# Delta-rule diagonal blocks inverted by columns on VectorE, with block doubling from 16

## The chip, the cores and the metric

The kernel runs on one core of a Trainium2 chip. The metric is the device time of one execution in microseconds (us), as the median of several runs. The profile that is read below comes from one further execution of the same program.

## What is computed

The reference is one mixer layer over 2048 tokens of width 1024. A normalised input goes through one projection. Half of its columns feed a gated delta rule (4 heads of 128), the other half feed differential softmax attention (4 heads). Both outputs are gated, concatenated and projected back to the residual stream. The change touches only the delta rule's triangular solve:

```
m    = where(strict, einsum('bhncd,bhnsd->bhncs', k_beta, kc) * decay, 0)
lmat = m + eye(CHUNK)
sol  = triangular_solve(lmat, rhs, left_side=True, lower=True, unit_diagonal=True)
u, w = sol[..., :dv], sol[..., dv:]
```

The kernel works with chunks of 128 tokens. It forms the inverse of the unit-triangular matrix explicitly and multiplies by it.

## The kernel before

The program has two stages. In the first, TensorE projects the input (the products named `pct` and `pnat`, each of them split into high and low parts, so three products for one), and beside this the delta rule runs. In the second, attention runs beside the output projection (`outp`).

The delta rule is cut into 16 units: 4 heads h by 4 token groups g of 512 tokens, each with 4 chunks (`NCH`). Two chains of units run abreast, one for even and one for odd groups, so that the two units of one head and one half of the tokens go through together; here they are called a pair, and there are 8 pairs. A third chain, the scans, carries the state from chunk to chunk.

`gdn_unit` builds the strictly upper triangle `U` of a unit, transposes it on TensorE (`lp`) into `L`, and then inverts. It starts with the inverse `N` of the 2x2 diagonal blocks, which needs only a mask, and doubles the block size at each level: a product with `Lr` (`xp`), masked by VectorE into `X`, a product with `TT` (`np`), which VectorE subtracts from `N`, and a transposition of `N` on TensorE (`tp`), which ScalarE copies into `TT`. With `LEVELS = [1, 2, 4, 8, 16, 32, 64]` there are six such rounds, for 2 to 64. One residual step (`rp`, `R`, `cp`, `NF`) follows, and then the products with keys and values (`wp`, `ubp`).

The order on TensorE is made by `mingle`, which takes one step of the delta rule at a time and puts steps of the projections behind it, on average `RATE` of them for each step, so that TensorE has work while the delta rule waits for the other engines. A projection step may be moved forward past at most `SLACK` = 4 delta-rule steps; within that freedom the framework's scheduler fixes the order of each engine's queue when the program is built. Each engine then works through its queue in order.

SyncE issues nearly all transfers, in one queue and in order. GpSimd (POOL) does the subtractions that make the low parts of the weights (`wl_...`), some elementwise work, and a few transfers at the start.

Of the kernel before, what the change touches and what calls it, by code (L numbers as in the profile page):

```python
# [10 lines left out]
F32 = mybir.dt.float32  # L11
F32R = mybir.dt.float32r
AF = mybir.ActivationFunctionType
ALU = mybir.AluOpType
AX = mybir.AxisListType

P = 128
# [6 lines left out]
NCH = 4  # L24
# [9 lines left out]
LD = 3  # L34
WB = 4
ORDER = ((0, 0, 1, 1), (0, 0, 1, 1))
RATE = 5.25
RATE_T = 5.25
RATE_D = 5.25
SLACK = 4  # L40
LOWER = [(h, g) for h in (0, 1, 2, 3) for g in (0, 1, 2, 3)]
LASTG = (4, 5, 6, 7)
# [22 lines left out]
EXB = 14  # L65
WTB = 4

LEVELS = [1, 2, 4, 8, 16, 32, 64]


def level_masks():
    s = np.arange(P)[:, None]
    c = np.arange(P)[None, :]
    m = [((s // (2 * b) == c // (2 * b)) & (s // b % 2 == 0) & (c // b % 2 == 1)) for b in LEVELS]
    return np.ascontiguousarray(np.stack(m, 1).astype(np.float32))


def f(ap):
    return ap.bitcast(F32)
# [3 lines left out]
def hybrid_kernel(  # L83
# [20 lines left out]
    nc = tc.nc  # L104
    V, A, PL, SY = nc.vector, nc.scalar, nc.gpsimd, nc.sync
# [41 lines left out]
    const = ctx.enter_context(tc.tile_pool(name="const", bufs=1))  # L147
    dram = ctx.enter_context(tc.tile_pool(name="dram", bufs=1, space=bass.MemoryType.DRAM))
# [6 lines left out]
    def qt_(name):  # L155
        return psf.tile([P, NCH, P], F32, tag="qt", name=name, bufs=1)
# [12 lines left out]
    mx_d = [[dram.tile([2, 8, P, G], F32, name=f"mx_d{g}")] for g in range(T // G)]  # L169
    zdn_d = [dram.tile([P, T], F32, name=f"zdn_d{h}") for h in range(H)]  # L170
    part_d = [dram.tile([P, D], F32, name=f"part_d{i}") for i in range(T // P)]
    gc_d = [dram.tile([H, 8, P], F32, name=f"gc_d{i}") for i in range(2)]

    xp = p1.enter_context(tc.tile_pool(name="xp", bufs=1))
# [2 lines left out]
    gp = pg.enter_context(tc.tile_pool(name="gp", bufs=1, side="right"))  # L177
# [51 lines left out]
    ident = const.tile([P, P], F32, name="ident")  # L229
# [4 lines left out]
    V.memset(ones, 1.0)  # L234
    utri = const.tile([P, P], F32, name="utri")
    PL.affine_select(utri, ones, pattern=[[1, P]], compare_op=ALU.is_ge, fill=0.0, base=0, channel_multiplier=-1)
    lmask = const.tile([P, 7, P], F32, name="lmask")
    ab = const.tile([P, 2, H], F32, name="ab")
    nea = const.tile([P, H], F32, name="nea")
    dtb = ab[:, 1, :]  # L240
    lv = const.tile([P, 1], F32, name="lv")

    ngp = qt_("ngp")
    PE.transpose(ngp[:, 0, 0:8], ngt, ident[0:8, 0:8])
    ngain = const.tile([P, 8], F32, name="ngain")
# [46 lines left out]
    def ua(gg, name, dt=F32):  # L292
        return psg.tile([P, NCH, P], dt, tag=f"ua{gg}", name=name, bufs=1)
# [263 lines left out]
    solved = [0]  # L557
    scanned = [0]

    def gdn_unit(h, g):  # L560
        u = units.pop((h, g))
        hf, gg = g // 2, g % 2
        kq, vT = u["kq"], u["vT"]
        s = {k: a[:, h, 4 * gg : 4 * gg + 4] for k, a in sc[hf].items()}

        def t(tag, name, dt=F32, shape=S4):
            return gp.tile(shape, dt, tag=f"u{gg}_{tag}", name=f"u{gg}_{name}")

        def live(name):
# [5 lines left out]
            out=gcr.rearrange("p a b -> p (a b)"),  # L575
            in_=gc_d[hf][h, 4 * gg : 4 * gg + 4, :].rearrange("a b -> (a b)").partition_broadcast(P),
# [46 lines left out]
        U = t("d", "U")  # L623
# [13 lines left out]
        passed[0] += 1  # L637


        lp = ua(gg, "lp")  # L640
        for j in range(NCH):
            PE.transpose(lp[:, j, :], U[:, j, :], ident)
        idb = bc(ident.unsqueeze(1), S4)
        L = t("a", "L")
        V.tensor_tensor(L, lp, idb, op=ALU.add)
        Lr = t("b", "Lr", F32R)
        A.copy(Lr, L)

        def lm(i):
            return bc(lmask[:, i, :].unsqueeze(1), S4)  # L650

        n0 = t("e", "n0")
        PL.tensor_tensor(n0, U, lm(0), op=ALU.mult)
        N = t("c", "N", F32R)
        PL.tensor_tensor(N, idb, n0, op=ALU.subtract)

        def transposed(N):
            tp = ua(gg, "tp", F32R)
# [5 lines left out]

        TT = transposed(N)
        yield
        for i in range(1, 7):

            def odd(a):
                return a.rearrange("p j (m two b) -> p j m two b", two=2, b=LEVELS[i])[:, :, :, 1, :]  # L670

            def blocks(a):
                return a.rearrange("p j (m b) -> p j m b", b=LEVELS[i])

            No = odd(N)
            HC = P // 2
            xp_ = ua(gg, "xp")[:, :, :HC]
            for j in range(NCH):
                PE.matmul(xp_[:, j, :], lhsT=Lr[:, j, :], rhs=No[:, j], start=True, stop=True)
            X = t("e", "X", F32R)[:, :, :HC]  # L680
            V.tensor_tensor(blocks(X), blocks(xp_), odd(lm(i)), op=ALU.mult)
            yield
            np_ = ua(gg, "np")[:, :, :HC]
            for j in range(NCH):
                PE.matmul(np_[:, j, :], lhsT=TT[:, j, :], rhs=X[:, j, :], start=True, stop=True)
            V.tensor_tensor(No, f(No), blocks(np_), op=ALU.subtract)
            yield
            TT = transposed(N)
            yield
# [101 lines left out]

    pace = [RATE]

    def feed():

        for hf in range(2):
# [23 lines left out]
            if hf:  # L820
                pace[0] = RATE_T
            for r in rest:
# [439 lines left out]
def build(arrays):  # L1262
    import concourse.bacc as _bacc

    nc = _bacc.Bacc("TRN2", target_bir_lowering=False, num_devices=1)
    args = []
    for name, a in arrays.items():
        args.append(nc.dram_tensor(name, a.shape, mybir.dt.from_np(a.dtype), kind="ExternalInput").ap())
    args.append(nc.dram_tensor("out_0_dram", (1, T, D), F32, kind="ExternalOutput").ap())
    with tile.TileContext(nc, schedule_with_timeline_sim=True) as tc:  # L1270
        hybrid_kernel(tc, *args)
    return nc
# [10 lines left out]
```

## Time and profile before

| what | value |
|---|---|
| median of 3 runs | 1722.77 us (1721.42 to 1725.84) |
| the profiled execution | 1718.26 us |
| its span, first to last instruction | 1716.1 us |
| mean granted TensorE clock, share of full speed | 0.984 |
| busy, share of the span: TensorE products | 95% |
| VectorE, ScalarE, POOL | 62%, 44%, 40% |

The profiled execution took 2.2 us more than its span, and 4.5 us less than the median of the three runs. Busy times of TensorE are modelled, since its products overlap; the distance between the starts of neighbouring products is the better measure of what one costs.

### The profile page before, as it was taken

The page shows a single profiled execution, that of the slowest core. Times are in us where ns is not written, and L with a number is a line of the kernel's source. Part 1 is how long each engine was busy: PE and PEld are TensorE (multiplying, and loading weights), DVE is VectorE, ACT ScalarE, POOL GpSimd, SP SyncE. Part 2 cuts the span into 40 slices and gives each one's busy share as a digit, 9 for nine tenths or more (in the row PEclk, how much of TensorE's full clock was granted, in tenths as well). Part 3 has the DMA queues.
Part 4 walks back from the last instruction along what each step waited for, and adds up shares of the span by engine and source line. Part 5 has one row for each costly group of instructions (what it writes and reads, how often), then busy time and mean ns, then how long its engine had stood idle before and what let it go on. Part 6 is the DMA issues. An engine that isn't in the chain of part 4 may idle for free.

```text
span 1716.1 us, 28068 instructions
## 1 busy us (share of the span) xinstructions
PE 1622.8 (95%) x9900; PEld 1414.1 (82%) x9900; DVE 1066.1 (62%) x2435; ACT 751.6 (44%) x2153; POOL 680.7 (40%) x789
## 2 busy tenths in 40 slices
PE   6999999999999899999999999989999989999987
PEld 5788899898988888889989898868777867778766
DVE  4765655645444486556573643337888778888772
ACT  5333333333334343433342333236777656565530
POOL 3454374253242256327344144022334354343432
PEclk9999999999999899999999999999999999999998
DMA  8232244233234341323313232596743364543343
GB/s 175 62 93 74 44 90 101 62 93 56 62 99 103 71 125 61 83 66 72 114 43 106 37 62 75 139 285 201 198 139 117 121 192 149 167 143 101 119 151 135
DMA packets 186969, 188.16 MB, mean 110 GB/s; under 512 B 12242, under 2 KB 142412, under 8 KB 186828
## 3 DMA queue, kind: packets, MB, share of 16 engines
q1 hardware_dynamic: 186556, 185.78, 39.5%
q8 instruction: 78, 1.28, 0.3%
q0 software_dynamic: 272, 0.59, 0.2%
q14 instruction: 63, 0.52, 0.1%
HBM read 124.42 MB, written 61.90 MB: 109 GB/s over the span
## 4 chain that ended last, share of the span: by engine, by line
PE 75%; DVE 8%; DMA 7%; ACT 4%; POOL 3%; issue 2%; SPq 1%; DVEq 0%; POOLq 0%; ACTq 0%
PE pct L113 24%; PE pnat L113 15%; PE outp L113 7%; PE oT L113 6%; PE sp L113 5%; PE wtp L116 2%; DVE nm L940 2%; PE xp L113 2%; DVE ex L994 2%; PE np L113 2%; PE tp L116 2%; DMA wr_fqk<-in_w_in_dram 2%; PE gqp L113 2%; ACT ex L942 1%; PE op L113 1%
## 5 line engine op out<-in xcount | busy, mean ns | idle before, releaser
L942 ACT ACTIVATE ex<-sp,nm 128x512 f32<-128x512 f32 (+3 forms) x320 | 198.5, 625 | 94.2 <-DVE nm L940 82.8
L113 PE MATMUL outp<-wo,mt 128*128 128x512 f32 x720 | 202.4, 414 | 5.2 <-ACT wo L1119 2.1
L940 DVE TENSOR_REDUCE nm<-sp 128x1 f32<-128x512 f32 (+3 forms) x320 | 186.3, 600 | 27.2 <-PE sp L113 25.6
L113 PE MATMUL sp<-k,qs 128*128 128x512 f32 (+3 forms) x640 | 184.4, 392 | 19.0 <-ACT ex L942 18.1
L113 PE MATMUL pnat<-wh_fqk,xh 128*128 128x256 f32 (+1 forms) x512 | 152.9, 300 | 16.0 <-ACT wh_fqk L336 8.8
L113 PEld LDWEIGHTS outp<-wo,mt 128*128 128x128 f32 x720 | 131.4, 193 | 31.4 <-ACT xr L1193 3.0
L113 PE MATMUL pnat<-wl_fqk,xh 128*128 128x256 f32 (+1 forms) x512 | 151.4, 297 | 1.6 <-POOL wl_fqk L337 1.6
L113 PE MATMUL pnat<-wh_fqk,xl 128*128 128x256 f32 (+1 forms) x512 | 150.1, 295 | 0.0
L113 PEld LDWEIGHTS sp<-k,qs 128*128 128x128 f32 x640 | 106.6, 190 | 49.6 <-ACT ex L942 37.5
L113 PE MATMUL oT<-wt,v 128*128 128x256 f32 (+1 forms) x576 | 132.7, 375 | 0.0
L528 DVE SCALAR_TENSOR_TENSOR cy<-craw,cc,cy 128x512 f32<-128x512 f32 x144 | 122.8, 853 | 3.3
L990 POOL TENSOR_SCALAR ex<-ex,al 128x512 f32<-128x512 f32 (+3 forms) x140 | 98.2, 716 | 61.4 <-ACT al L951 60.9
L113 PEld LDWEIGHTS oT<-wt,v 128*128 128x128 f32 x576 | 109.0, 193 | 16.2 <-ACT wt L1000 0.5
L994 DVE SCALAR_TENSOR_TENSOR ex<-ex,cf 128x512 f32<-128x512 f32 (+3 forms) x160 | 112.7, 743 | 12.9 <-ACT cf L969 10.0
L662 ACT CAST u_TT<-tp 128x512 fp32r<-128x512 f32 x112 | 65.5, 587 | 117.7 <-PE tp L116 117.6
L113 PEld LDWEIGHTS pnat<-wh_fqk,xh 128*128 128x128 f32 x512 | 99.7, 195 | 18.3 <-ACT wh_fqk L336 10.4
L113 PE MATMUL pct<-xh,wh_dvz 128*128 128x512 f32 x256 | 103.8, 406 | 0.0
L113 PE MATMUL pct<-xh,wh_dqk 128*128 128x512 f32 x256 | 103.5, 405 | 0.0
L113 PE MATMUL pct<-xl,wh_dvz 128*128 128x512 f32 x256 | 103.1, 403 | 0.0
L113 PE MATMUL pct<-xh,wl_dvz 128*128 128x512 f32 x256 | 103.0, 403 | 0.0
L113 PEld LDWEIGHTS pnat<-wl_fqk,xh 128*128 128x128 f32 x512 | 100.0, 195 | 3.3 <-POOL wl_fqk L337 3.0
L113 PE MATMUL pct<-xl,wh_dqk 128*128 128x512 f32 x256 | 102.6, 401 | 0.0
(271 smaller groups left out, 4179.4 us busy)
## 6 DMA issues: line engine op xcount, KB each, us to landing
qs<-qst_d SPq DMA_DIRECT2D x128, 128.0 KB, 3.1
mt<-mx_d SPq DMA_DIRECT2D x48, 256.0 KB, 4.0
k<-kst_d SPq DMA_DIRECT2D x40, 256.0 KB, 5.4
wr_dqk<-in_w_in_dram SPq DMA_DIRECT2D x32, 256.0 KB, 5.7
wr_dvz<-in_w_in_dram SPq DMA_DIRECT2D x32, 256.0 KB, 5.7
qst_d<-qkhl SPq DMA_DIRECT2D x16, 512.0 KB, 2.8
kst_d<-qkhl SPq DMA_DIRECT2D x16, 512.0 KB, 3.4
part_d<-xr SPq DMA_DIRECT2D x32, 256.0 KB, 3.7
```

Source lines behind the costliest of these rows:

```text
L113: last[0] = nc.tensor.matmul(*a, **k)
L116: last[0] = nc.tensor.transpose(*a, **k)
L528: V.scalar_tensor_tensor(y, raw[:, j : j + G], convc[:, j, idx : idx + 1], y, op0=ALU.mult, op1=ALU.add)
L662: A.copy(TT, f(tp))
L940: V.tensor_reduce(mx, sp[:, :w], axis=AX.X, op=ALU.max, negate=True)
L942: A.activation(e[:, :w], sp[:, :w], AF.Exp, bias=mx, accum_out=ss[:, m, pi : pi + 1])
L990: PL.tensor_scalar(e0[:, :w], e0[:, :w], al[:, 0, pi : pi + 1], 1.0, op0=ALU.mult, op1=ALU.mult)
L994: V.scalar_tensor_tensor(e1[:, :w], e1[:, :w], cf[:, pi : pi + 1], e0[:, :w], op0=ALU.mult, op1=ALU.add)
```

## The change

The diagonal blocks of 16x16 are now inverted before the doubling, which keeps only the levels 16, 32 and 64. POOL masks `U` to its diagonal blocks (`ud`), VectorE folds the 128 columns to 16 (`uc`, 128x64 for the four chunks). The folded triangle is written to DRAM (`ub_d`) and read back so that each of the 16 partitions of a block holds the whole block (`Ub16`, 4 KB on each partition). When the second unit of a pair has come so far, VectorE runs 15 column steps of two instructions each on both units together: `x` = row times column, and `nb` = `nb` - `x`. Their free size is 8 times 15, 14, ... 1. POOL then spreads the result into `N` with a mask. The first unit of a pair waits for the second. `RATE` (with `RATE_T` and `RATE_D`) goes from 5.25 to 6.1; a unit has fewer steps now.

```
-LEVELS = [1, 2, 4, 8, 16, 32, 64]
+B0 = 16
+NB = P // B0
+LEVELS = [16, 32, 64]
...
+        ud = t("e", "ud")
+        PL.tensor_tensor(ud.rearrange("p j (r c) -> p j r c", c=B0), U.rearrange("p j (r c) -> p j r c", c=B0), m16, op=ALU.mult)
+        uc = t("uc", "uc", shape=[P, NCH, B0])
+        V.tensor_reduce(uc, ud.rearrange("p j (r c) -> p j c r", c=B0), axis=AX.X, op=ALU.add)
+        SY.dma_start(out=ub_d[gg].rearrange("r (k e) -> (r k) e", k=B0), in_=uc.rearrange("p j c -> p (j c)"))
+        SY.dma_start(
+            out=pair["U"][:, gg],
+            in_=ub_d[gg].unsqueeze(1).to_broadcast([NB, B0, NCH * B0 * B0]),
+        )
...
-        n0 = t("e", "n0")
-        PL.tensor_tensor(n0, U, lm(0), op=ALU.mult)
+        if second:
...
+            for k in range(B0 - 1):
+                S = [P, 2, NCH, B0 - 1 - k]
+                x = gp.tile([P, 2, NCH, B0 - 1], F32, tag="x16", name="x16", bufs=1)[:, :, :, : B0 - 1 - k]
+                V.tensor_tensor(x, ub[:, :, k, :, k + 1 :], bc(nb[:, :, :, k : k + 1], S), op=ALU.mult)
+                V.tensor_tensor(nb[:, :, :, k + 1 :], nb[:, :, :, k + 1 :], x, op=ALU.subtract)
+                if k % 3 == 2:
+                    yield
+            pair["N"] = nb
+        while "N" not in pair:
+            yield "wait"
         N = t("c", "N", F32R)
-        PL.tensor_tensor(N, idb, n0, op=ALU.subtract)
+        PL.tensor_tensor(
+            N.rearrange("p j (r c) -> p j r c", c=B0),
+            bc(pair["N"][:, gg].unsqueeze(2), S5),
+            m16,
+            op=ALU.mult,
+        )
...
-        for i in range(1, 7):
+        for i in range(len(LEVELS)):
```

The change also makes the mask tile smaller, adds a small constant `ic16`, and sets aside less memory for transfers issued by POOL.

How the queues change is seen at the first pair. On TensorE, the program before goes from the second unit's `lp` straight to a transposition of `N`:

```order
L113 MATMUL pnat<-wl_fqk_0_1125,xh_416 128x256
L113 MATMUL pnat<-wh_fqk_0_1124,xl_417 128x256
L116 MATMUL lp<-ident,u_U 128x128 x4
L116 MATMUL tp<-identr,u_N 128x128 x4
L113 MATMUL pnat<-wh_fqk_0_1128,xh_416 128x256
L113 MATMUL pnat<-wl_fqk_0_1129,xh_416 128x256
```

In the changed program the first `tp` stands far behind that `lp`, after projections and transpositions `qktp` of other work. These are its last neighbours:

```order
L117 MATMUL pct<-xh_225,wh_dqk_0_1687 128x512
L117 MATMUL pct<-xl_226,wh_dqk_0_1687 128x512
L120 MATMUL qktp<-ident,qkraw 128x128 x4
L120 MATMUL tp<-identr,u_N 128x128 x4
L117 MATMUL pct<-xh_225,wl_dqk_0_1688 128x512
L117 MATMUL pct<-xh_225,wh_dqk_0_1694 128x512
```

Between the second `lp` and this `tp` there are now 53 `pnat`, 11 `pct` and 12 single `qktp`; before there was nothing.

On VectorE at the same place, before, after the sums `L` come the doubling steps `X` and `N`, with other work (`qkraw`, `qkss`, `qkhl`) between:

```order
L645 TENSOR_TENSOR u_L<-lp,ident 128x512 x2
L681 TENSOR_TENSOR u_X<-xp,lmask 128x4x64
L686 TENSOR_TENSOR u_N<-u_N,np 128x128x2
L465 TENSOR_TENSOR qkraw<-qkraw,qkr 128x256 x4
L458 TENSOR_REDUCE qkss<-qksq 128x4
L681 TENSOR_TENSOR u_X<-xp,lmask 128x4x64
L474 SCALAR_TENSOR_TENSOR qkhl<-qktp,qg,qkhl 128x512
L686 TENSOR_TENSOR u_N<-u_N,np 128x64x4
```

Now the fold `uc` stands behind `L`, three to five other instructions follow, and then the columns begin (`Ub` is the tile read back, `Nb` the columns of the inverse):

```order
L669 TENSOR_TENSOR u_L<-lp,ident 128x512
L658 TENSOR_REDUCE u_uc<-u_ud 128x64
L465 TENSOR_REDUCE qkss<-qksq 128x4
L481 SCALAR_TENSOR_TENSOR qkhl<-qktp,qg,qkhl 128x512
L465 TENSOR_REDUCE qkss<-qksq 128x4
L481 SCALAR_TENSOR_TENSOR qkhl<-qktp,cc,qkhl 128x512
L465 TENSOR_REDUCE qkss<-qksq 128x4
L687 TENSOR_TENSOR x_1506<-Ub_1449,Nb_1504 128x120
L688 TENSOR_TENSOR Nb_1504<-Nb_1504,x_1506 128x8x15
L687 TENSOR_TENSOR x_1509<-Ub_1449,Nb_1504 128x8x14
```

So what stands behind the first column instruction on VectorE now waits for the read from DRAM as well. In SyncE's queue, before, loads of weights and writes of `qkhl` follow each other there:

```order
L499 DMA zdn_d_81<-zz 128x512
L330 DMA wr_dvz_0_1708<-in_w_in_dram 128x4x128 x2
L475 DMA qst_d_68<-qkhl 128x2x512
L475 DMA kst_d_64<-qkhl 128x2x512
L330 DMA wr_dvz_0_1719<-in_w_in_dram 128x4x128 x2
```

The changed program has the two writes and the two reads of the folded triangles between them, each read behind a wait for its write:

```order
L506 DMA zdn_d_81<-zz 128x512
L337 DMA wr_dvz_0_1702<-in_w_in_dram 128x4x128 x2
L659 DMA ub_d_101<-u_uc 128x64
L659 DMA ub_d_102<-u_uc 128x64
L660 DMA Ub_1449<-ub_d_101 128x1x1024
L660 DMA Ub_1449<-ub_d_102 128x1x1024
L482 DMA qst_d_68<-qkhl 128x2x512
L482 DMA kst_d_64<-qkhl 128x2x512
L337 DMA wr_dvz_0_1713<-in_w_in_dram 128x4x128 x2
```

The writes of `qkhl` and the next load of weights therefore stand behind two transfers that wait for VectorE and for each other.

## Rows read from the trace of the kernel before

**Rows 1.** Busy times by stretch: span, engines, granted clock, DMA share, GB/s.

```profile
131.00:1097.00 966.00, 943.12 (x6328) 850.67 (x6327) 527.57 (x1105) 348.97 (x907) 390.65 (x394) 0.99 0.31 77
1097.00:1140.00 43.00, 34.53 (x195) 28.43 (x194) 16.32 (x41) 12.29 (x34) 13.62 (x12) 0.88 0.97 253
```

**Rows 2.** Chain that ended last: start, length, work; two stretches of projections.

```profile
62.74 11.11 PE pct L113 x48
...
266.71 8.49 PE pnat L113 x71
```

**Rows 3.** The same chain from the last projection to the free-running output projection.

```profile
1095.97 0.56 PE pct L113 x2
...
1126.82 6.07 DMA wor<-in_w_out_dram
...
1137.04 3.05 PE outp L113 x12
```

**Rows 4.** Timeline of TensorE: start us, length us, engine, line, instruction.

```profile
723.21 0.46 PE L116 MATMUL tp<-identr,u_N 128*128 128x128 f32 x4
723.50 0.46 PE L113 MATMUL pct<-xh,wh_dqk 128*128 128x512 f32 x1
723.80 0.40 PE L113 MATMUL pct<-xl,wh_dqk 128*128 128x512 f32 x1
...
726.25 0.53 PE L113 MATMUL xp<-u_N,u_Lr 128*128 128x64 f32 x4
726.61 0.48 PE L113 MATMUL pct<-xl,wh_dqk 128*128 128x512 f32 x1
726.93 0.39 PE L113 MATMUL pct<-xh,wl_dqk 128*128 128x512 f32 x1
```

**Rows 5.** Timeline of one unit: POOL's mask product, TensorE's transposition of `U`.

```profile
247.13 1.32 POOL L653 TENSOR_TENSOR u_n<-u_U,lmask 128x512 f32<-128x512 f32 x1 [0.31 <-DVE u_U L633]
...
249.93 0.60 PE L116 MATMUL lp<-ident,u_U 128*128 128x128 f32 x4
```

**Rows 6.** Groups of VectorE, 131 to 1097 us: busy, mean ns, idle before.

```profile
L528 DVE SCALAR_TENSOR_TENSOR cy<-craw,cc,cy 128x512 f32<-128x512 f32 x126 | 105.0, 834 | 2.8
...
L465 DVE TENSOR_TENSOR qkraw<-qkraw,qkr 128x256 f32<-128x256 f32 x56 | 28.3, 565 | 12.9 <-POOL qkr L462 12.9
...
L458 DVE TENSOR_REDUCE qkss<-qksq 128x4 f32<-128x256 f32 x52 | 21.5, 413 | 14.8 <-POOL qksq L457 14.3
```

**Rows 7.** Timeline of a write to DRAM, its read back, and the reader.

```profile
96.62 0.33 SPq L424 DMA_DIRECT2D gc_d<-gts  x1
98.06 0.86 SPq L574 DMA_DIRECT2D u_gcr<-gc_d  x2
...
101.47 1.24 ACT L579 ACTIVATE u_egr<-u_gcr 128x512 f32<-128x512 f32 x2 [2.29 <-DMA u_gcr<-gc_d]
```

**Rows 8.** VectorE, dependent small instructions (timeline), and one larger group (ns min/median/max).

```profile
66.68 0.19 DVE L403 TENSOR_TENSOR ts_pl<-ts_pl,ts_s 128x32 f32<-128x32 f32 x1
66.91 0.18 DVE L404 TENSOR_SCALAR ts_pl<-ts_pl 128x32 f32<-128x32 f32 x1
...
L583 DVE TENSOR_TENSOR u_df<-u_gcr,ts_gcl x16: 691/692/1785, 101.5 to 1009.5; 128x512 f32<-128x512 f32 x16
```

**Rows 9.** Timelines of VectorE and POOL over the same stretch.

```profile
721.18 0.75 DVE L528 SCALAR_TENSOR_TENSOR cy<-craw,cc,cy 128x512 f32<-128x512 f32 x1
722.03 1.30 POOL L337 TENSOR_TENSOR wl_dvz<-wr_dvz,wh_dvz 128x512 fp32r<-128x512 f32 x1 [0.85 <-ACT wh_dvz L336]
722.27 3.44 DVE L528 SCALAR_TENSOR_TENSOR cy<-craw,cc,cy 128x512 f32<-128x512 f32 x2
```

**Rows 10.** Busy times and granted clock around two idle times of TensorE.

```profile
555.00:564.50 9.50, 0.67 (x7) 0.46 (x5) 0.03 (x1) 0.73 (x2) 0.02 (x1) 0.76 0.92 175
564.50:570.00 5.50, 5.50 (x25) 5.50 (x26) 2.19 (x5) 4.22 (x9) 3.26 (x3) 0.50 0.38 60
...
41.00:44.50 3.50, 3.50 (x17) 3.23 (x17) 2.75 (x7) 2.46 (x7) 0.00 (x0) 0.51 0.22 87
```

More of the change, by code (lines that the diff above doesn't have):

```diff
@@ L36 @@
 ORDER = ((0, 0, 1, 1), (0, 0, 1, 1))
-RATE = 5.25
-RATE_T = 5.25
-RATE_D = 5.25
+RATE = 6.1
+RATE_T = 6.1
+RATE_D = 6.1
 SLACK = 4
@@ L74, in level_masks @@
     m = [((s // (2 * b) == c // (2 * b)) & (s // b % 2 == 0) & (c // b % 2 == 1)) for b in LEVELS]
+    m.append((s // B0 == c // B0) & (s <= c))
     return np.ascontiguousarray(np.stack(m, 1).astype(np.float32))
@@ L171, in hybrid_kernel @@
     part_d = [dram.tile([P, D], F32, name=f"part_d{i}") for i in range(T // P)]
+    ub_d = [dram.tile([NB, B0 * NCH * B0], F32, name=f"ub_d{i}") for i in range(2)]
     gc_d = [dram.tile([H, 8, P], F32, name=f"gc_d{i}") for i in range(2)]
@@ L236, in hybrid_kernel @@
     PL.affine_select(utri, ones, pattern=[[1, P]], compare_op=ALU.is_ge, fill=0.0, base=0, channel_multiplier=-1)
-    lmask = const.tile([P, 7, P], F32, name="lmask")
+    lmask = const.tile([P, len(LEVELS) + 1, P], F32, name="lmask")
+    ic16 = const.tile([P, B0], F32, name="ic16")
     ab = const.tile([P, 2, H], F32, name="ab")
@@ L241, in hybrid_kernel @@
     lv = const.tile([P, 1], F32, name="lv")
+    V.tensor_reduce(ic16, ident.rearrange("p (r c) -> p c r", c=B0), axis=AX.X, op=ALU.add)
     ngp = qt_("ngp")
@@ L558, in hybrid_kernel @@
     scanned = [0]
+    pairs = {}
     def gdn_unit(h, g):
@@ L637, in gdn_unit @@
         passed[0] += 1
+        pair = pairs.setdefault((h, hf), dict(n=0))
+        if "U" not in pair:
+            pair["U"] = gp.tile([P, 2, NCH * B0 * B0], F32, tag="Ub16", name="Ub16")
+        S5 = [P, NCH, NB, B0]
+        m16 = bc(lmask[:, len(LEVELS), :].rearrange("p (r c) -> p r c", c=B0).unsqueeze(1), S5)
+        ud = t("e", "ud")
[7 more added lines that the diff above has]
+        )
         lp = ua(gg, "lp")
@@ L647, in gdn_unit @@
         A.copy(Lr, L)
+        pair["n"] += 1
+        second = pair["n"] == 2
+        yield
         def lm(i):
             return bc(lmask[:, i, :].unsqueeze(1), S4)
-        n0 = t("e", "n0")
-        PL.tensor_tensor(n0, U, lm(0), op=ALU.mult)
-        N = t("c", "N", F32R)
-        PL.tensor_tensor(N, idb, n0, op=ALU.subtract)
+        if second:
+            ub = pair["U"].rearrange("p g (k j c) -> p g k j c", k=B0, c=B0)
+            nb = gp.tile([P, 2, NCH, B0], F32, tag="Nb16", name="Nb16")
+            V.tensor_copy(nb.rearrange("p g j c -> p (g j) c"), bc(ic16.unsqueeze(1), [P, 2 * NCH, B0]))
+            for k in range(B0 - 1):
[4 more added lines that the diff above has]
+                if k % 3 == 2:
+                    yield
+            pair["N"] = nb
+        while "N" not in pair:
+            yield "wait"
+        N = t("c", "N", F32R)
+        PL.tensor_tensor(
[4 more added lines that the diff above has]
+        )
         def transposed(N):
@@ L1263, in build @@
     import concourse.bacc as _bacc
-    nc = _bacc.Bacc("TRN2", target_bir_lowering=False, num_devices=1)
+    nc = _bacc.Bacc("TRN2", target_bir_lowering=False, num_devices=1, dynamic_dma_scratch_size=4096)
     args = []
```

## The prediction

> **What bounds the kernel now.** I read the busy times by stretch first. Between 131 us, where the first unit's triangle is transposed, and 1097 us, where the last projection ends, TensorE is busy 943 of 966 us at a granted clock of 0.99, while VectorE is busy for 528 and POOL for 391 [rows 1]. So this stage goes at TensorE's pace, and a product less is time less, as long as no new wait is put in its place. The chain of work that ended last says the same and gives the price of a projection: 48 `pct` in 11.11 us are 0.231 us each, 71 `pnat` in 8.49 us are 0.120 us each [rows 2]. From the last `pct` at 1096.5 us to the output projection that runs freely at 1137 us, the chain goes through loads of its weights (`wor`, 6.07 us for one), and the DMA engines are busy 0.97 of that stretch [rows 1, 3]. These 41 us begin when the projections end, whatever the delta rule does in them. Attention, behind it, is not touched. What counts is therefore the stage from 131 to 1097 us.
>
> **What is removed.** Three rounds of doubling for each of 16 units, 48 groups of four each of `tp`, `xp` and `np`. A group costs the time to the next `pct`, and what the distance to the one after exceeds 0.231 us. For `tp`: 0.29 us and 0.07 us, together 0.36. For `xp`: 0.36 and 0.09, together 0.45 [rows 4]. `np` has the same shapes as `xp`. A round is 0.36 + 2 x 0.45 = 1.26 us, and 48 rounds are 60.5 us. VectorE loses 96 instructions, ScalarE 48 copies, and neither sets the pace.
>
> **What is added beside other work.** POOL's two products `ud` and `N` take the place of two products of the same shape, at 1.3 us [rows 5]. VectorE's fold of 512 elements I price from the sum over 256 at 0.413 us [rows 6] and a slope per element: 0.19 us at 32 elements and 0.692 at 512 [rows 8], 1.045 ns each, so 0.41 + 0.27 = 0.68 us. In sum VectorE gets a few tens of us more on 528 of 966 and does not become the bound. That is hidden by TensorE's work, as long as nobody waits.
>
> **What is added on the path.** Between `U` and the first `tp` of a pair, TensorE now has only the projections that the queue puts there. Counted in the order, from the second `lp` to the first `tp`, and priced by [rows 2] (transpositions and small products at 0.12), the eight pairs have 10.4, 24.7, 20.7, 15.0, 7.6, 24.9, 20.9 and 15.2 us. Against these stands a chain of waits:
>
> 1. The fold. In the trace POOL's product on `U` starts 2.8 us before `lp` [rows 5]. In pairs 1, 2, 3 and 6 the order has the fold behind `L`, which waits for `lp`: 0.1 + 0.69 + 0.68, so 1.5 us after the end of `lp`, 1.9 in pairs 2 and 6, where one `y` more stands between. In pairs 4, 7 and 8 the fold comes ahead of `L` and ends about 1 us before. In pair 5 both units come together and POOL makes one `ud` after the other: 0.5 us.
> 2. Through DRAM. The nearest thing in the trace is the write of `gts`, 16 KB: issued at 96.62 us, its read could be issued at 98.06, and the reader of 256 KB started at 101.47, so 1.4 and 3.4 us [rows 7]. The new write has 32 KB, the read 512 KB. The further 256 KB at the 253 GB/s of [rows 1] are 1.0 us. I take 1.4 + 4.4 = 5.8 us, and 7.8 in pairs 1 and 5, whose two reads run together. The lower bound is 4.8, as in the row; the upper is 2 us more.
> 3. The columns. 30 instructions, each of which needs the one before. At no elements an instruction takes 0.19 - 32 x 1.045 ns = 0.157 us; two times 8 x (15 + 14 + ... + 1) = 1920 elements add 2.0 us; start to start is 0.035 us more than the length [rows 8]. 4.7 + 2.0 + 1.05 = 7.8 us. They read two operands from SBUF, as `cy` does, which in this stage takes 0.834 us on average [rows 6] and 0.75 alone [rows 9], 11% more. So 8.7 us. The lower bound is 30 x 0.19 = 5.7; the upper one is a rival below.
> 4. Others' instructions inside the columns, by the order. Pairs 1 and 5: four `qkraw` of 0.565, one or two sums of 0.413 [rows 6], a small one: 2.9 and 3.3 us. Pairs 2 and 6: 12 of `cy`'s kind at 0.75, four `qkraw`, three single-operand passes and one normalisation of the same size at 0.5 to 0.7, some small ones: 14.5, of which I take off 1 us, as they fill the gaps between dependent columns: 13.5. Pairs 4 and 8: 3.1. Pairs 3 and 7: none.
> 5. POOL's `N` and its signals: 1.4 us.
>
> Sums: pair 1, 1.5 + 7.8 + 8.7 + 2.9 + 1.4 = 22.3 against 10.4, a stall of 11.9. Pair 5, 21.7 against 7.6: 14.1. Pairs 2 and 6, 31.3 against 24.8: 6.5 each. Pairs 3 and 7, 17.4 at most against 20.8: none. Pairs 4 and 8, 18.0 against 15.1: 2.9 each. Together 44.8 us. In `SyncE`'s queue the weights behind the read wait up to 6 us with it; I cost that at nothing, since three raw tiles and POOL's and ScalarE's work lie between a load and its product, and if that cover were gone it would be those 6 us, in four pairs at most.
>
> **The clock.** [...] Pairs 1 and 5 at 2.75, the four smaller stalls at 1.7: 12.3 us.
>
> **Sum.** -60.5 + 44.8 + 12.3 = -3.4 us. The profiled execution (1718.3 us, 1716.1 of it span) would come to 1714.9; the median of the runs shown is 4.5 us higher, so 1722.8 - 3.4 gives 1719 us. A measurement of this kernel tells a change of 0.3%, 5 us, from none.
>
> **Rivals.** *The waits are mostly covered.* With every column at 0.19 us and no blocking (5.7), and the read as quick as the row's (1 us less), each chain is 4 us shorter. Stalls: 7.9, 10.1, 2 x 2.5, none in the rest, 23 us; clock 2 x 2.75 + 2 x 1.7 = 8.9. -60.5 + 31.9 = -29 us: 1694. For it: the smallest rows are real ones, and the last columns have only 8 elements. Against it: the larger ones do have more.
>
> *POOL stops the columns.* In [rows 9] two `cy` take 3.44 us, where 1.5 would do, while POOL subtracts weights for 1.30 us. The columns are thirty chances for POOL to come in. In pairs 1, 2, 5 and 6 POOL has about four such subtractions queued there, in the others two. If each holds up the columns for its whole length, they take 7.8 + 5.2 = 13.0 us, or 10.4, which is 4.3 and 1.7 more than I took. Stalls: 16.2, 18.4, 2 x 10.8, 2 x 4.6, 65.4 us; clock 4 x 2.75 + 2 x 1.7 = 14.4. -60.5 + 79.8 = +19 us: 1742, slower. It decides from 1.4 us more per stalled pair on, when the 3.4 us and the 0.3% are used up. Against it: the average of `cy` over the stage is only 11% longer. [...]
>
> *The removed products do not set the time.* Then the stage would keep its 966 us: TensorE's idle 23 us in it leave no room for more than those, so at most -60.5 x 0.976 becomes real instead of 60.5, 1.5 us. I give it nothing of its own. What could happen is that the two last units, which now end together, leave their scans to run alone; they have the 41 us of weight loads to hide in.
>
> **From the cases to the numbers.** The forecast, between -15 and +10 us: 0.42. Covered waits, -15 to -45: 0.28. Stopped columns, +10 to +35: 0.25. Something in VectorE's queue that starves the projections, slower still: 0.05. Of the forecast's 0.42 I put 0.16 below -5 us, 0.18 within and 0.08 above. Faster: 0.28 + 0.16 = 0.44. Same: 0.18. Slower: 0.08 + 0.25 + 0.05 = 0.38. The range takes in the sums of both rivals, 1694 and 1742, with the little that their bounds add: 1690 to 1746. The forecast's own range is 1708 to 1733, its -15 to +10.
>
> **What would show it.** In the changed profile the groups `tp`, `xp` and `np` have 256, 192 and 192 products. TensorE's idle times of more than 5 us stand at the first `tp` of pairs 1, 2, 5 and 6, ended through POOL's `N`, with a granted clock of 0.5 behind them; pairs 3 and 7 have none. The write and read take 5 to 8 us, the columns 8 to 9 us in pairs 3 and 7, where nothing stands between them. The prediction is wrong if the columns there take 11 us or more (the POOL rival), if pairs 1 and 5 stall less than 8 us (the covered one), if the stretch behind the last projection is not 41 us, or if TensorE waits at `pct` or `pnat` for a free result bank while VectorE waits for DRAM.

## The result, and the profile after

The changed kernel takes 1753.36 us (1749.37 to 1755.54, four runs) where the kernel before took 1723.08 (1721.42 to 1725.84, four runs): a ratio of 1.0171 (95% interval 1.0149 to 1.0194). It is 1.7% slower, which is clear of the noise, 34 us above the forecast of 1719 and outside the range of 1690 to 1746.

First the busy times by stretch of the changed kernel, the rows that answer to [rows 1]. I cut at the first `lp`, the last `pct` and the first product of attention, which now come at 137.1, 1115.1 and 1179.0 us (before: 131.1, 1096.1, 1143.7). Columns as in [rows 1]: the stretch and its length; busy time and instructions of TensorE's products, TensorE's weight loads, VectorE, ScalarE and POOL; granted clock, DMA share, GB/s.

```profile
137.00:1115.00 978.00, 903.62 (x5754) 802.81 (x5752) 560.85 (x1272) 323.00 (x859) 387.85 (x394) 0.97 0.38 85
1115.00:1179.00 64.00, 51.14 (x247) 41.78 (x247) 15.95 (x40) 14.92 (x38) 14.96 (x13) 0.84 0.87 236
1179.00:1752.00 573.00, 524.27 (x2689) 426.70 (x2687) 439.21 (x1092) 331.03 (x1057) 211.06 (x308) 0.97 0.49 148
```

In the stage of the projections TensorE has some 570 products fewer, but is idle for 74 us in place of 23, at a clock of 0.97 in place of 0.99. The stage is 13 us longer, not 3 shorter. And the loss does not lie there alone: the span grew by 36 us, 6 of them before the first `lp`, 13 in the stage, 17 behind the last projection.

What TensorE waited for in the stage: engine, line, product, releaser; us in total, times, longest.

```profile
PE tp L120 <- POOL u_N L695: 16.3, 7, 3.9
PE qktp L120 <- DVE qkraw L472: 14.9, 5, 12.4
PE qktp L120 <- DVE Nb L688: 13.7, 1, 13.7
PE pnat L117 <- ACT wh_fqk L343: 11.2, 1, 11.2
PE otp L120 <- DVE on L797: 5.7, 6, 1.4
```

The kernel before has two of these rows, the fourth (at the start of the third group of tokens) and a small second:

```profile
PE pnat L113 <- ACT wh_fqk L336: 8.8, 1, 8.8
PE qktp L116 <- DVE qkraw L465: 3.5, 5, 1.1
```

The first three rows of the changed kernel, 44.9 us, are new but for these 3.5 us, and nearly all lie between a pair's second `lp` and its first `tp`. The largest two, in pairs 1 and 5, end not at `tp` but at `qktp`. Pair 1 shows why, in the timelines of SyncE, VectorE, POOL and TensorE:

```profile
142.19 1.88 SPq L659 DMA_DIRECT2D ub_d<-u_uc  x2
144.18 1.83 SPq L660 DMA_DIRECT2D Ub<-ub_d  x2
...
142.67 1.03 DVE L658 TENSOR_REDUCE u_uc<-u_ud 128x64 f32<-128x512 f32 x1
...
155.77 0.28 DVE L687 TENSOR_TENSOR x<-Ub,Nb 128x120 f32<-128x120 f32 x1 [7.78 <-DMA Ub<-ub_d]
...
159.96 0.17 DVE L467 TENSOR_SCALAR qkss<-qkss 128x16 f32<-128x16 f32 x1
...
163.14 1.09 DVE L472 TENSOR_TENSOR qkraw<-qkraw,qkr 128x256 f32<-128x256 f32 x3
...
164.77 0.17 DVE L688 TENSOR_TENSOR Nb<-Nb,x 128x8 f32<-128x8 f32 x1
...
160.21 2.90 POOL L469 TENSOR_TENSOR qkr<-qkss,mhalf 128x16 f32<-128x16 f32 x1 [7.13 <-DVE qkss L467]
165.03 2.49 POOL L695 TENSOR_TENSOR u_N<-Nb,lmask 128x512 fp32r<-128x512 f32 x2 [1.92 <-DVE Nb L688]
...
163.71 1.47 PE L120 MATMUL qktp<-ident,qkraw 128*128 128x128 f32 x4 [12.35 <-DVE qkraw L472]
166.34 0.75 PE L120 MATMUL tp<-identr,u_N 128*128 128x128 f32 x4 [1.15 <-POOL u_N L695]
```

VectorE stands for 7.8 us at the first column, which waits for the read. Behind it in VectorE's queue, after seven of the fifteen column steps (4.2 us from the first column to it), stands `qkss`. POOL's `qkr` waits for `qkss`, VectorE's `qkraw` waits for `qkr`, and TensorE's `qktp` waits for `qkraw`. I had counted that `qktp` as cover, that is, as work for TensorE during the wait; it was itself behind the columns.

The clock around this idle time, in the same columns as [rows 1]:

```profile
151.00:163.70 12.70, 0.35 (x2) 0.02 (x1) 7.10 (x31) 0.00 (x0) 4.97 (x4) 0.69 0.80 157
163.70:169.50 5.80, 4.64 (x14) 3.26 (x15) 2.19 (x8) 1.27 (x2) 2.49 (x2) 0.50 0.24 90
169.50:173.00 3.50, 3.50 (x23) 3.07 (x22) 1.18 (x2) 1.56 (x3) 0.00 (x0) 1.00 0.13 50
```

As in [rows 10], the granted clock is 0.50 behind the idle time, for 5.8 us, and then 1.00 again.

### The profile page after: what moved, and what is told of

Same layout as the page of the kernel before. It is cut to its first block, busy times and chain, and to the rows that moved or that the text cites. A ratio compares the mean times of both kernels' runs of the same rounds, so it can differ in the third digit from the quotient of the medians.

```text
span 1752.1 us, 27017 instructions
## 1 busy us (share of the span) xinstructions
PE 1590.8 (91%) x9324; PEld 1368.8 (78%) x9324; DVE 1098.4 (63%) x2604; ACT 724.7 (41%) x2105; POOL 674.9 (39%) x789
## 5 line engine op out<-in xcount | busy, mean ns | idle before, releaser
L117 PE MATMUL outp<-wo,mt 128*128 128x512 f32 x720 | 204.8, 418 | 12.4 <-ACT wo L1164 6.0
L117 PE MATMUL oT<-wt,v 128*128 128x256 f32 (+1 forms) x576 | 131.1, 370 | 0.4 <-ACT wt L1045 0.2
L1035 POOL TENSOR_SCALAR ex<-ex,al 128x512 f32<-128x512 f32 (+3 forms) x140 | 94.4, 689 | 83.8 <-ACT al L996 83.4
L117 PE MATMUL pct<-xh,wl_dqk 128*128 128x512 f32 x256 | 104.8, 412 | 0.2 <-POOL wl_dqk L344 0.2
```

The source lines that it names most:

```text
L117: last[0] = nc.tensor.matmul(*a, **k)
L1035: PL.tensor_scalar(e0[:, :w], e0[:, :w], al[:, 0, pi : pi + 1], 1.0, op0=ALU.mult, op1=ALU.mult)
```

## The experiments

**How they are compared.** Every kernel's span is split in the same way, and the edits are given in short. *Start* is the time to the first `lp`, *stage* from there to the last `pct`, *end* from there to the end of the span. The distance from the start of each of TensorE's products to the start of the next is divided into three parts. Up to the median distance of such a pair of products in the kernel before (at most 0.6 us) it is work; while the granted clock is at its lower level, up to 0.9 of that more is *clock*; the rest is *waiting*. The last two are given for the stage. Spans are those of one profiled execution, medians and ratios those of the timed runs.

| kernel | median us | ratio to before (95%) | start | stage | waiting | clock | end |
|---|---|---|---|---|---|---|---|
| before | 1723.08 | | 131.1 | 965.0 | 68 | 2 | 620.0 |
| changed | 1753.36 | 1.0171 (1.0149 to 1.0194) | 137.1 | 978.0 | 121 | 16 | 637.0 |
| e5_no_read_wait | 1724.47 | 1.0018 (1.0004 to 1.0032) | 137.2 | 946.4 | 96 | 11 | 641.5 |
| e6_one_column | 1707.96 | 0.9916 (0.9884 to 0.9948) | 137.9 | 935.5 | 85 | 11 | 635.9 |
| e7_neither | 1688.18 | 0.9803 (0.9769 to 0.9836) | 138.3 | 916.6 | 72 | 5 | 631.7 |
| e4_removal_alone | 1663.87 | 0.9646 (0.9621 to 0.9671) | 139.0 | 901.3 | 63 | 2 | 623.6 |
| e12_pairing_alone | 1744.63 | 1.0110 (1.0055 to 1.0165) | 129.0 | 979.6 | 83 | 6 | 633.0 |
| e10_units_alone | 1775.02 | 1.0311 (1.0290 to 1.0333) | 136.4 | 1012.5 | 141 | 31 | 623.8 |
| e13_last_pair_alone | 1754.25 | 1.0183 (1.0151 to 1.0215) | 136.4 | 981.5 | 127 | 16 | 634.5 |
| e11_more_cover | 1756.07 | 1.0209 (1.0173 to 1.0245) | 136.6 | 983.5 | 125 | 17 | 633.1 |
| e3_old_rate | 1822.86 | 1.0592 (1.0567 to 1.0616) | 135.6 | 1046.7 | 169 | 24 | 638.3 |
| e14_blocks_of_8 | 1727.13 | 1.0024 (1.0008 to 1.0040) | 135.2 | 966.6 | 101 | 11 | 622.6 |
| e16_blocks_of_8_placed | 1730.14 | 1.0033 (1.0018 to 1.0048) | 134.9 | 970.9 | 100 | 16 | 624.5 |
| e9_masks_placed_as_before | 1751.18 | 1.0164 (1.0144 to 1.0185) | 136.8 | 977.1 | 121 | 15 | 632.0 |
| e15_tile_of_512_bytes | 1754.36 | 1.0172 (1.0146 to 1.0198) | 136.2 | 978.9 | 120 | 18 | 634.6 |
| e20_mask_tile_as_before | 1760.03 | 1.0193 (1.0138 to 1.0249) | 138.1 | 984.7 | 121 | 22 | 637.6 |
| e1_scratch_alone | 1723.31 | 1.0012 (0.9993 to 1.0030) | 130.3 | 968.7 | 70 | 5 | 621.9 |
| e17_before_shifted | 1722.40 | 0.9989 (0.9973 to 1.0006) | 130.1 | 969.3 | 69 | 6 | 625.7 |
| e18_dram_tiles | 1723.76 (one run) | | 131.1 | 968.6 | 69 | 5 | 621.9 |
| e19_sbuf_room | 1720.94 (one run) | | 130.8 | 965.6 | 69 | 3 | 622.7 |

The last four rows and before have one order of the queues (but for an instruction or two transfers that are added), e9, e15, e20 and the changed kernel another. They give the spread, 4 us in the stage and 6 in the end for the first order, 8 and 6 for the second, and means: start 130.7 and 137.1, stage 967.4 and 979.7, end 622.4 and 635.3. By these the changed kernel loses 6, 12 and 13 us, 31 in sum, as the medians have it (30.3).

**The chain, taken apart.** Three variants of the changed kernel leave out the wait for the read, most of the columns, or both.

```
e5:  -  ub = pair["U"].rearrange("p g (k j c) -> p g k j c", k=B0, c=B0)
     +  ub = bc(pair["uc"].unsqueeze(2), [P, 2, B0, NCH, B0])   # uc: both units' folds in one tile
e6:  +  if k == 0:      # around the two instructions of a column
e7:  both
```

> The changed kernel, whose columns multiply by the folded triangle itself (one row for all sixteen) and not by the tile read back; the write and the read are still made, and only nobody waits for them. Theory A (waits for chain and columns, about 53 us of waiting and 14 us of clock in the stage of the projections): the chain is 8 to 12 us shorter in each pair, about 28 us of the waits and 7 of the clock go, 1718 us. Rival B (the transfers burden SyncE's queue and delay the weights behind them): the time stays within 10 us of the changed kernel's 1753. Rival C (the projections' new pace, not the chain, costs the time): it stays too.

> The changed kernel with one column step of fifteen; 14 steps, 28 instructions a pair, are left out. Theory A: the chain is about 8 us shorter in each pair, and 10 to 18 where other work stands between the columns; about 33 us of the waits and 9 of the clock go, 1711 us, with the waits that are left in pairs 1 and 5 (about 8 us each). Rivals B and C: within 10 us of 1753.

> The changed kernel with both edits: one column step of fifteen, and it reads the folded triangle itself. Theory A: nearly all of the waits and of the lost clock go, 50 and 12 us: 1691 us, and what is left above before minus the removed rounds (1723 - 53 = 1670) is the start and the tail behind the last projection, some 22 us. Rivals B and C: the time stays above 1735.

Measured were 1724, 1708 and 1688 us, against 1718, 1711 and 1691 expected by theory A and 1735 or more by the rivals, which fall: the waits for the read and for the columns cost the time. What the waits are then, in e6 and in e7:

```profile
PE tp L120 <- POOL u_N L696: 11.1, 2, 6.0
```

```profile
PE pnat L117 <- ACT wh_fqk L343: 11.0, 1, 11.0
PE qktp L120 <- DVE qkhl L481: 4.6, 4, 2.1
PE otp L120 <- DVE on L800: 4.4, 4, 1.4
```

With one column only pairs 1 and 5 still wait at `tp`. With neither, no wait at `tp` is left among the largest, and the stage is 61 us shorter than in the changed kernel (978.0 - 916.6).

**The removal alone.**

```
-  the fold, its transfers, the pairing, the columns
+  N = t("c", "N", F32R)
+  PL.tensor_tensor(N, idb, ud, op=ALU.subtract)
   RATE, RATE_T, RATE_D: 6.1 -> 6.9
```

> The three removed rounds alone: N is the unit triangle with the sign of its 16x16 blocks turned (a first-order inverse, in place of the columns' exact one), from POOL's mask product as before; no fold, no transfers, no columns, no pairing; 6.9 projections for a step, so that 48 output products stand ahead of attention, as in the kernel before. Masks, constant and the memory for POOL's transfers as in the changed kernel. Theory A: 55 us less of products in the stage of the projections (894 us at their usual distances before, 839 to 841 in the variants of the changed kernel), no more waits than before: 1668 us, or 1674 if the first lp comes 6 us late here too. The prediction's own price was 60.5 us: 1662. On the loads: if the packets of 512 bytes take 43 ns here, the fold's transfers or tiles slow them; if 59, the masks, the constant and POOL's memory together do.

The stage is 63.7 us shorter than before, the whole 1663.87 us, a ratio of 0.9646. The prediction's price of the three rounds was 60.5 us. The time expected was 1668 us, or 1674 with the late start that e4 does have (139.0 us). So the gain is real, and e4's 1664 us are what the method would have to come near to. They price the rounds only: e4 leaves out the work that would replace them, and its N is not the one that the columns make.

**The pairing.** e7 has no columns to speak of and waits for no read, but is 24 us slower than e4: 15 in the stage, 8 in the end. What it still has is the pairing, the fold and the transfers. It also has another pace than e4 (6.1 in place of 6.9) and 84 output products ahead of attention in place of 48, so the 15 us are not the pairing's alone. The pairing by itself is tried in the kernel before:

```
+  pair = pairs.setdefault((h, hf), dict(n=0))
+  pair["n"] += 1
+  while pair["n"] < 2:
+      yield "wait"
   N = t("c", "N", F32R)
```

> The kernel before, with the pairing alone: the first unit of a pair waits with its N until the second has come so far. All seven levels, no fold, no columns, the old pace. Theory G (the pairing moves the scans of the two last units behind the last projection, and this lengthens the end): the stage of the projections stays within 8 us of before's 965, the stretch from the last projection to the end grows from 620 us to 632 or more, 1733 us or more. Rival: the end grows through what else the change does (the pace, the memory of tiles), and this run is as fast as before within 5 us.

It costs 21 us by the medians (its four runs lie between 1733.6 and 1751.1): the stage is 12 us longer than the mean of the five runs with the order of before, the end 11. The end is as theory G has it; that the stage would stay was wrong. TensorE's largest waits in its stage, beside that for `wh_fqk`:

```profile
PE ysp L113 <- DVE y L737: 5.9, 6, 1.4
PE ubp L113 <- ACT nw L713: 3.4, 6, 0.7
PE np L113 <- DVE u_X L687: 2.3, 4, 0.9
```

They are many and small, and the stage has 83 us of waiting where before and its variants have 68 to 70. My reading is that two units at the same step want the same engines at the same time, so that one no longer works in the other's waits; no run shows that this is the reason.

Without pairs, and with the last pair alone unpaired:

```
e10: U16, nb and x for each unit, 15 columns on half the elements; RATE 5.6
e13: alone = (h, hf) == (H - 1, 1);  if second or alone: ... on this unit's half
```

> No pairs: each unit has its own columns, with half the elements, and waits for no other; 5.6 projections for a step, so that as much is left behind the last projection as before the change (48 output products ahead of attention, as in the kernel before). Theory A: a unit's chain is 1 + 8.3 + 6.8 + 1.4 = 17.5 us, of which the other unit's steps cover a part; the waits in the stage of the projections fall below those of the changed kernel by 20 us or more, and the tail to about 48 us: 1715 to 1735 us. Rival F (VectorE's 240 further column instructions and the sixteen waits in place of eight cost what pairing saved): 1750 us or more.

> The changed kernel, in which the two units of the last pair alone don't wait for each other; each has its own columns. By the order 48 output products stand ahead of attention, as in the kernel before (96 in the changed one). Theory G: the stretch from the last projection to the end falls from 637 us to about 622, the rest stays: 1738 us. Rival: it falls by less than 5 us, since what attention gains by starting earlier it pays for with the output products that are left for later (as in the run with four empty steps, where the tail was 14 us shorter and attention 10 us longer): 1750 us.

e10 has the short end (623.8 us), but sixteen waits in place of eight: 141 us of waiting and 31 of clock in the stage, 1775 us, as rival F said. Theory A had 1715 to 1735. In e13 the busy times show that the tail itself shrank, and that attention took it back:

```profile
1118.00:1166.00 48.00, 38.90 (x211) 32.25 (x210) 17.14 (x42) 14.00 (x36) 14.75 (x13) 0.86 0.97 261
1166.00:1752.00 586.00, 531.13 (x2739) 435.39 (x2737) 441.24 (x1092) 333.89 (x1061) 215.00 (x309) 0.98 0.50 149
```

48 us up to attention in place of 64, but 586 of attention in place of 573: the output products that the changed kernel had done early, 48 by the order, stand in it now. Theory G, which had 1738 us, fell here; the rival held.

**The pace.**

```
e11: +  for _ in range(4 if second else 0):
     +      yield                 # ahead of the columns; RATE 5.6
e3:  RATE, RATE_T, RATE_D: 6.1 -> 5.25
```

> The changed kernel with four empty steps of the delta rule ahead of the columns of each pair, behind which projections are put, and 5.6 of them for a step. By the order the cover of the pairs is 13, 25, 18, 19, 13, 20, 20 and 21 us (10, 25, 21, 15, 8, 25, 21, 15 in the changed kernel), and 48 output products stand ahead of attention in place of 96. Theory A: 5 us less of waits in the stage of the projections, a tail of about 48 us in place of 64: 1735 us. Rival D (tail set by loads alone): the tail stays above 60 us and the time at 1748 or more.

> The changed kernel with the pace of before, 5.25 projections for a step of the delta rule in place of 6.1; nothing else. By the order on TensorE nothing of a unit is left behind the last projection, only the last scan, and the cover of the eight pairs (second lp to first tp) falls from 139 to 90 us in sum. Theory A (the tail is as long as what is left of the two last units): from the last projection to the first product of attention 48 us or less, 64 in the changed kernel; in the stage of the projections 35 to 50 us more of waits, since less covers them; together about 1775 us. Rival D (the tail is set by the loads of the output weights alone, whatever the delta rule does, and grew for another reason): it stays at 60 to 66 us.

e11 did not gain (1756 us where 1735 was expected): its tail, from the last projection to attention, is 50 us, as theory A said, but attention is 10 us longer for it, and the stage has 125 us of waiting in place of 121. With the old pace the stage waits 48 us more and attention is 49 us longer (622 in place of 573), as all output products are left for it; the price was higher than the 1775 us that I expected. Its tail is 16.5 us, so rival D, by which the loads alone set the tail, fell. The new pace was not the cause of the loss; it saved about 70 us.

**A smaller block.**

```
-B0 = 16                    +B0 = 8
-LEVELS = [16, 32, 64]      +LEVELS = [8, 16, 32, 64]
 RATE, RATE_T, RATE_D: 6.1 -> 5.75
```

> The same method with blocks of 8: seven columns in place of fifteen, a read of 128 KB in place of 512 KB for a unit, four levels of doubling in place of three (two rounds removed, not three), and 5.75 projections for a step. Theory A: two thirds of the removed 55 us, 37; the read 2 to 4 us shorter, the columns 3 to 4 us in place of 8.7, so waits of about 15 us in place of 46 at the first tp and half of the clock's loss: 1720 us, no slower than before. Rival (the latency of a transfer does not depend on its size, and the covers are shorter too): the waits stay above 35 us, 1740 us or more.

The kernel takes 1727.13 us. That is 26 us better than blocks of 16, with two rounds saved and not three, but still 0.24% slower than before (1.0008 to 1.0040) where 1720 us were expected. The rival fell: between the second `lp` and the first `tp` TensorE is idle for 20 us in the sum of the pairs, 53 in the changed kernel. The read has a quarter of the bytes, and more of its packets overlap. Here are VectorE's first column and SyncE's read, of pair 6 in e14:

```profile
814.14 0.52 SPq L660 DMA_DIRECT2D Ub<-ub_d  x1
...
816.56 0.56 DVE L687 TENSOR_TENSOR x<-Ub,Nb 128x56 f32<-128x56 f32 x1 [0.99 <-DMA Ub<-ub_d]
```

and, from the changed kernel, the hardware queue during a read, 245.0 to 248.4 us (packets, MB, share of 16 DMA engines):

```profile
q1 hardware_dynamic: 112, 0.46, 52.1%
```

The read of 512 KB keeps the 16 engines busy for about half of the time (52.1%): in single reads its 128 packets of 4 KB take 0.24 to 0.30 us each, 6.4 to 7.9 at once on average and 9 to 11 at most; the first starts 1.4 us after the issue, the last ends 5.3 to 6.7 us after it. In e14 about 20 overlap at most, and an undisturbed read of 128 packets of 1 KB ends 1.8 to 2.3 us after its issue. How much of e14's quicker read comes from the packets that overlap and how much from the fewer bytes is not shown: a read of the larger blocks in another shape was not tried.

**Where things lie.** Open were the 6 us at the start. They begin at `ab`, a small load by POOL, for which ScalarE waits longer in the changed kernel (first row) than in e18 (second row):

```profile
ACT nea L295 <- DMA ab<-in_a_log_dram: 8.2, 1, 8.2
```

```profile
ACT nea L289 <- DMA ab<-in_a_log_dram: 3.9, 1, 3.9
```

The loads of the first weights are under way then, and packets of 512 bytes, as the weights have them, are slower on average through the whole stage: 59 ns over the 43,072 packets from 60 to 1090 us in the changed kernel, 56 to 60 in every variant of it, 43 or 44 in the kernel before and its variants. The median packet takes 27 ns in both; the difference is made by few long ones, 2657 of 200 ns or more in the changed kernel and 645 before. Each of these runs undoes or does one thing that could be the cause:

```
e1:  before + dynamic_dma_scratch_size=4096
e9:  changed, level_masks: m += m[:3];  lmask loaded from masks[:, :4]
e15: changed, ic16 = const.tile([P, P], F32)[:, :B0]
e16: e14 with the same ic16
e17: before + gap = const.tile([P, 16], F32)
e18: before + two DRAM tiles of 32 KB at the place of ub_d
e19: before + dynamic_dma_scratch_size=4096 + gp.tile([P, 2304], F32)
e20: changed, lmask = const.tile([P, 7, P], F32)[:, :4]
```

> The kernel before, with the smaller memory for POOL's transfers alone. Theory A: this memory makes the first of POOL's loads (the tile ab, which landed 10.5 us after its issue in the changed kernel and 6.1 us in the one before) slower, and with it the 6 us that the changed kernel has lost by its first lp; then this run is 4 to 6 us slower than before, about 1728 us. Rival: the landing differs for another reason, and this run is as fast as before, within 2 us.

> The changed kernel, whose input of masks in DRAM has again seven of them, as before, of which the first four are loaded. Theory E: the six us lost by the first lp come from where the inputs lie in DRAM, since the same transfers before 45 us take longer in all kernels with the smaller mask input (137 to 138 us to the first lp in four of them, 130 to 131 in the kernel before and in the one with less memory for POOL's transfers): first lp at 131 us, 1747 us in all. Rival: it comes from the placing of tiles in SBUF or from elsewhere; first lp stays at 137 us, 1753 in all.

> The changed kernel, whose constant ic16 takes 512 bytes of a partition in place of 64, of which the first 64 are used; nothing else. Theory H: the new 64 bytes shift every tile behind them in SBUF, the raw weights among them, and their loads' packets of 512 bytes take longer for it (in the stage of the projections 59 ns a packet on average in the changed kernel and all its variants, 43 in the kernel before and its variants); with the shift a multiple of 512 again they take 43 ns, the first lp comes at 131 us in place of 137, and the time is 6 to 12 us below the changed kernel's 1753. Rival: the packets are slower for another reason (the transfers of the folded triangle between them), 59 ns and 1753 us.

> Blocks of 8 as in the run above with them, and the constant of 512 bytes. Theory H: 6 to 12 us less than that run's 1727: 1715 to 1721 us, 0.1 to 0.5% faster than the kernel before. Rival: 1727.

> The kernel before, with an unused constant of 64 bytes a partition at the place of ic16; the order of all queues is the same. Theory H: its packets of 512 bytes take 59 ns in place of 43 in the stage of the projections, the first lp comes at 137 us in place of 131, and the time is 6 us or more above before's 1723. Rival: 43 ns, 131 us, 1723 us.

> The kernel before with two more tiles of 32 KB in DRAM, at the place of ub_d (written once each, 16 KB beside the write of gts). If they move what the loads read or write in DRAM so that packets of 512 bytes take 59 ns in place of 43 and the first lp comes at 137 us, the place in DRAM is the cause; otherwise 43 ns and 131 us.

> The kernel before with the smaller memory for POOL's transfers and a tile of 9 KB a partition beside the delta rule's, set to zero once, as the changed kernel's Ub16 and its companions take it. If the packets of 512 bytes take 59 ns and the first lp comes at 137 us, the place in SBUF is the cause; otherwise 43 ns and 131 us.

> The changed kernel, whose tile of masks in SBUF has again seven places, as before, of which the first four are used; its input has four. Theory H2: the 1536 bytes by which the smaller tile moved all tiles behind it are what slows the packets of 512 bytes; with it they take 43 ns, the first lp comes at 131 us, and the time falls by the 6 us of the start, and by a few more, if the wait of 11 us at 571 us for the third group of tokens shrinks to the 9 us that it had: 1744 to 1748 us. Rival (the smaller input of masks, or the program itself): 59 ns, 137 us, 1753 us.

None moved it: 43 or 44 ns in e1, e17, e18 and e19, and 58 or 59 in e9, e15, e16 and e20, with starts as in the table. e4 has slow packets too (56 ns), without fold, transfers or columns. Theories E, H and H2 fell, and so did e1's theory A; the cause stays open, as do combinations of these. The wait for `wh_fqk`, 11.2 us in place of 8.8, is 11.0 in e4 too, so the transfers of the triangle are not what lengthened it.

## Why the prediction was wrong

**What it had right.** The removed rounds: 60.5 us forecast, 63.7 measured in the stage (e4). The counts of `tp`, `xp` and `np` are 256, 192 and 192. The columns: 8.7 us forecast, 8.8 in pairs 3 and 7. The clock, in sum: 12.3 us forecast, 14 measured (16 against 2). Place by place it was not right: behind pairs 1 and 5 it lost about 1.7 and 2.1 us and not 2.75, and 1.3 to 2.5 at seven further places where I had four. The terms of that sum, 2.75 and 1.7 us, were my estimate from [rows 10], 5.5 us at 0.50 and 3.5 us at 0.51; no run shows them at the places that I gave them. The stalls, nearly in sum: between the second `lp` and the first `tp` TensorE is idle for 15.2, 4.8, 3.7, 3.2, 16.5, 5.1, 1.4 and 2.9 us in pairs 1 to 8, together 52.8 against 44.8.

**Through DRAM** was mis-sized. From the end of the fold to the first column the eight pairs take 12.1, 9.5, 11.1, 8.5, 12.3, 8.7, 9.7 and 8.2 us, 80.1 in sum, where I had 5.8, and 7.8 twice, 50.4. The row that I took it from [rows 7] reads 256 KB at another shape. In the six pairs with single reads 3.5 us are missing on average; 2.6 of them lie between the read's issue and the first column, 0.9 ahead of the issue. The engines' idle half could explain most of the 2.6: from the first packet to the last it is 4.5 us on average, and by my estimate from the 52.1% it would be 2.3 us with all 16 engines busy. No run shows it. That the sum of the stalls came out within 8 us all the same is luck. From the second `lp` to the first `tp` the eight chains took 202.6 us where I had 177.4, although the columns of pairs 2 and 6 with the work between them took 19.5 and 19.1 us and not 22.2. Of these 25 us, 10.4 were covered, as the products between took longer than I had priced them, and 6.8 went into the slack of pairs 3 and 7. So pair 3 does stall at its first `tp` (2.6 us) where I had none, and pairs 2 and 6 wait there for 3.0 and 3.9 us where I had over 5. In pairs 1 and 5 the long wait is at `qktp` and not at `tp`, which I had not seen.

**The pairing had no term.** By the stages of e4, e7 and the changed kernel, 965.0 - 63.7 + 15.3 + 61.4 = 978.0: the removal, then what pairing, fold and transfers cost when nobody waits for the read and there is one column, then the waits for read and columns with their clock. The last, 61.4, is near my 44.8 + 12.3 = 57.1. The 15.3 us in the middle I had at nothing; they hold the difference in pace between e4 and e7 as well, and e12 shows the pairing alone at 12 in the other program. This term, left at nothing, is the step that turned the stage from -3 to +13.

**"Whatever the delta rule does"** was the second step that failed. From the last projection to the first product of attention it is 64 us and not 48 as before, and the whole end is 13 us longer by the means. That the stretch behind the last projection would change was one of my own signs of being wrong. Pairing in the kernel before lengthens the end by 11 (e12), and e4 and e10 without pairs have 624. But the last pair alone is not it (e13, 634.5), and blocks of 8 have a short end with pairs (e14, 622.6). What is shown is that the tail and attention trade output products, so that a shorter tail is no gain by itself (e11, e13). Attention in the changed kernel has 48 output products fewer to do than before, 11 us of work by the same split of distances, and takes as long (573.2 us, before 572.5), since 10 us more of waiting and 2 of clock stand in it. The largest row of waits behind the last projection, before and then changed, shows where most of this lies:

```profile
PE sp L113 <- ACT ex L942: 18.1, 35, 2.6
PE sp L117 <- ACT ex L987: 26.2, 38, 4.6
```

Why TensorE waits there longer for ScalarE, and so what makes the sum longer, is not settled.

**The start** was outside the argument, 6 us, cause open.

In the profiled spans the forecast missed by 39 us (-3.4 against +36.0). This is 15 for the pairing and what goes with it, 17 for the end, 6 for the start, and 4 more for waits and clock, less 3 that the removal gave beyond its price.

**The rivals.** The covered waits fell: pairs 1 and 5 stall for 15.2 and 16.5 us. That the removed products do not set the time fell with e4, whose stage is 63.7 us shorter. That POOL holds up the columns is real, but smaller than in the rival: in pair 3, between 402.45 and 403.80 us, POOL subtracts weights, and one column stands still as long (VectorE, then POOL):

```profile
402.42 0.24 DVE L688 TENSOR_TENSOR Nb<-Nb,x 128x80 f32<-128x80 f32 x1
402.69 1.21 DVE L687 TENSOR_TENSOR x<-Ub,Nb 128x72 f32<-128x72 f32 x1
403.93 0.23 DVE L688 TENSOR_TENSOR Nb<-Nb,x 128x72 f32<-128x72 f32 x1
...
402.45 1.35 POOL L344 TENSOR_TENSOR wl_dqk<-wr_dqk,wh_dqk 128x512 fp32r<-128x512 f32 x1 [11.69 <-ACT wh_dqk L343]
```

0.97 us over the median for its size. Of the 240 column instructions nine are held so by 0.4 to 1.1 us, 7.3 us in all, each beside an instruction of POOL on 256 or 512 elements (subtractions of weights, and once `qksq`). The length of POOL's instruction alone does not do it: `qkr` on 16 elements, 2.90 us in pair 1, held none of the eleven column instructions that ran within it. My 11% on 7.8 us stood for the one hold that pairs 3 and 7 have each, by chance. The rival counted up to four subtractions a pair; there were none to three within the columns. Its sum, 1742, lies nearer to the measured time than the forecast does, for another reason than the one it named: luck. The case that VectorE's queue starves TensorE, to which I gave 0.05, is what happens at `qktp` in pairs 1 and 5.

## What to carry to other kernels

A wait is priced with everything queued behind it on its engine: work counted as cover must not itself stand behind the wait, as the `qktp` of pairs 1 and 5 did (12.4 and 13.7 us). Joining two units so that one instruction serves both saves instructions on an engine with room to spare, but it is not free: tried alone (e12) it cost 12 us of the stage, a fifth of the 63.7 us that the removal gave, and 11 us behind it. I take the lost stagger between the units for the reason, which is not shown. Ask of a transfer on the path what share of the DMA engines it keeps busy before its bytes are divided by a rate: the 253 GB/s that I took come from a stretch with a share of 0.97 [rows 1], and the read had 52.1%.

## What the runs showed of the hardware that I had not expected

A read back from DRAM of 512 KB kept the 16 DMA engines busy for only 52.1% of the time and took 5.3 to 6.7 us from issue to last packet, one of 128 KB took 1.8 to 2.3 us. The sum over 512 elements to 64 takes 1.05 us, where the slope of the elementwise rows gave 0.68:

```profile
L658 DVE TENSOR_REDUCE u_uc<-u_ud 128x64 f32<-128x512 f32 x16 | 16.8, 1047 | 3.4 <-POOL u_ud L656 3.4
```

And the same weight loads took 59 ns a packet on average in one program and 43 in another, at the same median of 27 ns, for no reason found in eight runs. A long instruction of POOL on few elements (`qkr`, 2.90 us) held no column of VectorE, while each of the nine holds (0.4 to 1.1 us) lay beside one on 256 or 512.
